# Output projection: 512 columns and 128 tokens to a PSUM bank, in place of 256 columns and two times 128 tokens

## The chip, the cores and the metric

The kernel runs on one core of one Trainium2 chip. The metric is the device time of one execution in microseconds, from the first instruction to the last. Three runs of the kernel before gave 1098.61, 1100.31 and 1105.79 us; the median is 1100.31. The trace that is quoted here is that of another, profiled execution of the same kernel.

## What is computed

One layer of a hybrid encoder, on a prompt of 1024 tokens and a sample of 512 tokens, both of width 1024. A combined projection feeds a Hyena branch (short convolution, long convolution by transforms, gates) and a branch of neighbourhood attention with 8 heads of 64. Each branch gives 512 channels, and the layer ends in one output projection over both:

```python
def encoder_layer(x, norm_g, w_in, ...):
    h = rmsnorm(x, norm_g)
    z = h @ w_in
    ...
    y_hy = x0 * long_conv(x1 * vv, kfilt, hy_bias)
    y_hy = rmsnorm(y_hy, on_hy) * jax.nn.silu(hy_gate)
    ...
    y_att = neighbourhood_attention(q, k, v, rpb)
    y_att = rmsnorm(y_att, on_att) * jax.nn.silu(att_gate)
    return x + jnp.concatenate([y_hy, y_att], axis=-1) @ w_out
```

The change is in the last line alone. All values are float32.

## The kernel before

**Precision.** Products that need float32 are made of three matmuls on rounded halves: every operand is split into `hi` (rounded) and `lo` (the rest), and the sums hi x hi, hi x lo and lo x hi add up in PSUM. So each weight piece and each operand is loaded as float32, copied to `hi` (VectorE or ScalarE) and subtracted to `lo` (GpSimd).

**Stages.** The program goes through normalising and turning x, then the prompt's projections together with the filters' spectra, the prompt's Hyena, the prompt's attention together with the sample's Hyena, and last the output projection together with the sample's attention (`run`, lines 1148 to 1253). Within a stage, generators are traced in turns (`weave`, line 347) and a scheduler then sets the order of instructions on each engine by priorities; the attention of the sample has priority 4000 over the outputs. Each engine works in its order, so what waits at the head of its queue holds up all behind it. All DMAs are issued by SyncE (`dma`, line 58).

**The output projection** (`out_part`, lines 1078 to 1136). It runs in passes: part 0 multiplies the four channel blocks (k = 0 to 3, 128 channels each) of the Hyena output by their rows of `w_out`, part 1 does it for the attention. A job is 512 tokens: two jobs of the prompt and one of the sample. Part 0 of the prompt's two jobs comes first, then their part 1, then part 0 of the sample, and after the sample's attention has ended, part 1 of the sample. At the start of a pass each job loads its four operand blocks from scratch in DRAM (`lo<-A_p`, `lo<-A_s`, line 1089), ScalarE copies them to `hi` (line 1090) and GpSimd subtracts (`lo`, line 1091 through the helper at line 63). The operands have one tile per job and block, so part 1's loads wait until part 0 has let the tile go.

The loop inside (lines 1095 to 1136) takes 256 output columns at a time (g = 0 to 3). For each job and each pair of 128-token tiles it fills one PSUM bank of 512 float32: 4 blocks x 2 tiles x 3 matmuls of 256 columns = 24 matmuls. The token tile is the stationary operand, the weights stream:

```python
for g in range(4):                                                     # 1095
    ...
    units = [... self.take_w(("w_out", g, part)) ... for _ in range(2)]  # 1097
    for jb in jobs:
        ...
        for t in (0, 2):
            ps = self.bank(next(self.mm_tags)).rearrange("p (a c) -> p a c", a=2)
            for k in range(4):
                ...
                for j in range(2):
                    ...
                    for i, (w, h) in enumerate(((whi, hi), (wlo, hi), (whi, lo))):
                        nc.tensor.matmul(ps[:, j, :], lhsT=h[:, tok], rhs=w, ...)   # 1111
```

Then the bank is evicted, half by half. In job 0 and the sample's job VectorE adds it, scaled by each token's norm factor, to an accumulator in SBUF that was filled with x by DMA (`acc`, line 1133 through the helper at line 75). The prompt's second job has no accumulator: in part 0 ScalarE scales the bank (`oo`, line 1123) and a DMA writes it to DRAM scratch (`sum`), in part 1 `sum` and x come back (`oy`, `ox`), GpSimd adds them and VectorE adds the bank. In part 1 a DMA writes the output.

**The weights.** A piece is 128 partitions x 1024 columns (512 KB); for `w_out` that is 4 blocks x 256 columns. `fetch_w` (line 344 and after, DMA at line 351) loads it into one of two `wraw` tiles of a pool, `issue_w` (lines 354 to 367) splits it into two units of 512 columns, each with a `whi` (line 365) and a `wlo` (GpSimd, line 366), of which a pool has four each. `take_w` (line 369) hands units out in order and issues further pieces as far as there is room: `w_bufs` is 4 until part 0 of the prompt's jobs is done, then 8, and pieces go by turns to a second pool with the same number of tiles. One step of the loop over g uses one piece, two units.

**Attention of the sample** (line 894 and after). For each of 8 heads a table comes by DMA (`qkr<-in_rpb_dram`) and GpSimd makes two tables of it (`T`, then `Ti`). For each unit TensorE makes the scores (lines 994 and 995), VectorE and ScalarE the softmax, TensorE transposes (line 1020) and multiplies by the values (line 1029), ScalarE and VectorE put the result together (`ya`, lines 1033 and 1034). At the end of a pair of heads `finish` (line 1036) loads a gate (`qkr<-ga_s`), multiplies (line 1046) and stores the block to scratch (`A_s<-ya`). The row sums over channels (line 828) give the norm factors of part 1.

## Time and profile before

| | |
|---|---|
| median of three runs | 1100.31 us (1098.61 to 1105.79) |
| span of the profiled execution | 1101.3 us (the profile shows no time around it) |
| TensorE busy in it | 1030.7 us, 94%, 6492 matmuls |
| VectorE, ScalarE, GpSimd busy | 824.4, 561.1, 539.9 us |
| granted TensorE clock, mean | 0.987 of 2.4 GHz |
| DMA | 154.87 MB, 44.3% of the span of 16 engines |
| matmuls of the output projection (line 1111) | 1152, from 883.9 us to 1097 us |

The profile is one execution. A busy TensorE is not TensorE at its peak: matmuls are pipelined and their ends are modelled, so the distance between starts is the better measure. A wait is put down to the engine that released it last.

### The profile page before, as it was taken

How to read it: one execution, taken by the hardware profiler on the slowest of the kernel's cores; microseconds unless marked ns; L12 is line 12 of the kernel's file. 1: busy time of each engine (PE TensorE's matmuls, PEld its weight loads, DVE VectorE, ACT ScalarE, POOL GpSimd, SP SyncE). 2: the span in 40 equal slices, each digit the busy share in tenths (PEclk: the TensorE clock that was granted, in tenths of full speed). 3: DMA queues.
4: the chain of work that ended last, by engine and by line, in shares of the span. 5: the costliest groups of instructions: out<-in, count | busy, mean ns of one | idle time of the engine just before them, and what ended most of it. 6: DMA issues, size and time to landing. Idle time of an engine off the chain costs nothing. (4 is left out here: it accounts for less than half of the span.)

```text
span 1101.3 us, 18549 instructions
## 1 busy us (share of the span) xinstructions
PE 1030.7 (94%) x6492; PEld 895.6 (81%) x6492; DVE 824.4 (75%) x2098; ACT 561.1 (51%) x1223; POOL 539.9 (49%) x480
## 2 busy tenths in 40 slices
PE   3999898998999999999898999999999999899998
PEld 2888887987888878787786887888777798798898
DVE  5988679456148597868768898999886868966874
ACT  6644616444534343443425577667567764564530
POOL 2133636325245474545445645455455564766452
PEclk9999999899999999999999899999999999999999
DMA  9134461645612121122375244445544376966522
GB/s 343 34 122 144 143 207 61 219 150 164 224 39 74 46 79 54 50 72 77 118 227 173 78 129 146 120 141 182 140 129 138 114 243 190 321 203 205 164 76 89
DMA packets 110780, 154.87 MB, mean 141 GB/s; under 512 B 7793, under 2 KB 80315, under 8 KB 109919
## 3 DMA queue, kind: packets, MB, share of 16 engines
q1 hardware_dynamic: 110687, 153.69, 44.3%
q8 instruction: 51, 0.84, 0.3%
q14 instruction: 42, 0.34, 0.1%
HBM read 110.35 MB, written 43.32 MB: 140 GB/s over the span
## 5 line engine op out<-in xcount | busy, mean ns | idle before, releaser
L366 POOL TENSOR_TENSOR wlo<-wraw,whi 128x512 fp32r<-128x512 f32 x160 | 231.5, 1451 | 308.4 <-ACT whi L365 180.7
L392 PE MATMUL bank<-hThi_p,whi 128*128 128x512 f32 x320 | 125.2, 391 | 2.0 <-DVE cx L75 2.0
L392 PE MATMUL bank<-hTlo_p,whi 128*128 128x512 f32 x320 | 125.5, 392 | 0.0
L392 PE MATMUL bank<-hThi_p,wlo 128*128 128x512 f32 x320 | 125.4, 392 | 0.0
L405 PE MATMUL bank<-whi,hThi_p 128*128 128x256 f32 x384 | 110.4, 290 | 2.5 <-ACT qsq L849 2.0
L1111 PE MATMUL bank<-whi,hi 128*128 128x256 f32 x384 | 111.0, 291 | 0.8 <-ACT hi L1090 0.5
L405 PE MATMUL bank<-wlo,hThi_p 128*128 128x256 f32 x384 | 110.8, 291 | 0.0
L1111 PE MATMUL bank<-wlo,hi 128*128 128x256 f32 x384 | 110.0, 288 | 0.0
L1111 PE MATMUL bank<-whi,lo 128*128 128x256 f32 x384 | 109.5, 289 | 0.3 <-POOL lo L63 0.3
L405 PE MATMUL bank<-whi,hTlo_p 128*128 128x256 f32 x384 | 108.1, 289 | 0.0
L450 POOL TENSOR_TENSOR Z<-zc,Z 128x256 fp32r<-128x256 f32 x80 | 69.5, 878 | 49.2 <-ACT Z L449 36.2
L1002 ACT ACTIVATE s_sb<-s_sb,mx 128x360 f32<-128x360 f32 (+1 forms) x96 | 60.4, 629 | 63.6 <-DVE mx L998 63.0
L405 PEld LDWEIGHTS bank<-whi,hThi_p 128*128 128x128 f32 x384 | 74.2, 194 | 4.9 <-ACT qsq L849 2.4
L1111 PEld LDWEIGHTS bank<-whi,hi 128*128 128x128 f32 x384 | 73.4, 191 | 4.1 <-issue 2.1
L405 PEld LDWEIGHTS bank<-wlo,hThi_p 128*128 128x128 f32 x384 | 74.5, 194 | 1.6 <-issue 0.7
L1111 PEld LDWEIGHTS bank<-wlo,hi 128*128 128x128 f32 x384 | 73.6, 192 | 1.6 <-issue 1.6
L1111 PEld LDWEIGHTS bank<-whi,lo 128*128 128x128 f32 x384 | 73.1, 192 | 1.7 <-issue 1.1
L405 PEld LDWEIGHTS bank<-whi,hTlo_p 128*128 128x128 f32 x384 | 73.3, 194 | 1.2 <-issue 0.7
L392 PEld LDWEIGHTS bank<-hThi_p,whi 128*128 128x128 f32 x320 | 60.3, 188 | 14.0 <-DVE cx L75 2.4
L392 PEld LDWEIGHTS bank<-hTlo_p,whi 128*128 128x128 f32 x320 | 60.4, 189 | 11.3
L392 PEld LDWEIGHTS bank<-hThi_p,wlo 128*128 128x128 f32 x320 | 60.3, 188 | 11.3
L392 PE MATMUL bank<-hThi_s,whi 128*128 128x512 f32 x160 | 64.6, 407 | 4.4 <-DVE cvv L75 2.3
(292 smaller groups left out, 3108.4 us busy)
## 6 DMA issues: line engine op xcount, KB each, us to landing
wraw<-in_w_ch_dram SPq DMA_DIRECT2D x40, 512.0 KB
wraw<-in_w_tk_dram SPq DMA_DIRECT2D x24, 512.0 KB
wraw<-in_w_out_dram SPq DMA_DIRECT2D x16, 512.0 KB
V<-v_p SPq DMA_DIRECT2D x32, 240.0 KB
v_p<-vg SPq DMA_DIRECT2D x32, 160.0 KB
K_p<-Kw SPq DMA_DIRECT2D x4, 1088.0 KB
x<-in_x_prompt_dram SPq DMA_DIRECT2D x8, 512.0 KB
dec<-in_dec_p_dram SPq DMA_DIRECT2D x16, 256.0 KB
```

Source lines behind the costliest of these rows:

```text
L366: nc.gpsimd.tensor_tensor(out=lo, in0=r, in1=f32(hi), op=ALU.subtract)
L392: nc.tensor.matmul(ps, lhsT=w, rhs=h[s][:, k], start=(k == 0 and i == 0), stop=(k == KC - 1 and i == 2))
L405: nc.tensor.matmul(pss[t // 2][:, t % 2, :], lhsT=h[t // 4][:, k, t % 4 * P:(t % 4 + 1) * P], rhs=w, start=(k == 0 and i == 0 and t % 2 == ...
L450: nc.gpsimd.tensor_tensor(out=Z[:, 1, 0:2, :], in0=z, in1=f32(Z[:, 0, 0:2, :]), op=ALU.subtract)
L1002: nc.scalar.activation(out=s_sb[:, :n], in_=s_sb[:, :n], func=AF.Exp, bias=mx, scale=-1.0, accum_out=l)
L1111: nc.tensor.matmul(ps[:, j, :], lhsT=h[:, tok], rhs=w, start=(k == 0 and i == 0 and j == 0), stop=(k == 3 and i == 2 and j == 1))
```

## The change

A bank now holds one tile of 128 tokens and 512 output columns: 4 blocks x 3 matmuls of 512 columns = 12 matmuls in place of 24. The loop goes over two halves (h) of the output columns. Each half takes four units at its start, one unit per block k (512 columns of one block), and keeps them until its last tile. With two jobs, job 0 does its four tiles in the first step of the half and job 1 in the second, where before both jobs took turns in each of the four steps; with one job a step has two tiles. A bank is evicted by one operation of 512 columns. The piece of weights is now 2 blocks x 512 columns and is put together by two DMAs of 256 KB, since the weights lie in DRAM as before. Accumulators are filled with x by two loads of 1 MB in place of four of 512 KB. The number of banks (48) and the bytes are the same. Comments and docstrings also go.

```diff
         if what[:3] == "out":
-            return [[]] + [[("w_out", g, int(what[3]))] for g in range(4)]
+            return [[]] + [[("w_out", h, int(what[3]), u)] for h in range(2) for u in range(2)]
...
+    def load_w(self, raw, key):
+        if key[0] != "w_out":
+            self.dma(raw, self.io[key[0]][key[1:]])
+            return
+
+        _, h, part, u = key
+        for g in range(2):
+            self.dma(raw.rearrange("p (k g c) -> p k g c", k=2, g=2)[:, :, g],
+                     self.io["w_out"][h * 2 + g, part].rearrange("p (k c) -> p k c", k=4)[:, u * 2:u * 2 + 2])
+
     def fetch_w(self):
...
-            self.dma(raw, self.io[key[0]][key[1:]])
+            self.load_w(raw, key)
...
-        for g in range(4):
-            gs = slice(g * 256, (g + 1) * 256)
-            units = [[t.rearrange("p (k c) -> p k c", c=256) for t in self.take_w(("w_out", g, part))] for _ in range(2)]
...
+        for h in range(2):
+            hs = slice(h * 512, (h + 1) * 512)
+            units = [self.take_w(("w_out", h, part, k // 2)) for k in range(4)]
+            for step in range(2):
+                for jb in (jobs if len(jobs) == 1 else jobs[step:step + 1]):
+                    for t in (range(4) if len(jobs) > 1 else range(step * 2, step * 2 + 2)):
+                        self.out_tile(part, jb, t, hs, units)
+                yield
+
+    def out_tile(self, part, jb, t, hs, units):
+
+        nc = self.nc
+        G, acc = jb["G"], jb.get("acc")
+        t += jb["seg"] * 4
+        rows = slice(t * P, (t + 1) * P)
+        r = (G.ratt if part else G.rhy)[:, t:t + 1]
+        t %= 4
+        if part == 0 and acc and t == 0:
+            t0 = jb["seg"] * 4
+            self.dma(acc[:, :, hs], G.x[t0 * P:(t0 + 4) * P, hs].rearrange("(t p) c -> p t c", p=P))
+        ps = self.bank(next(self.mm_tags))
+        tok = slice(t * P, (t + 1) * P)
+        for k, (whi, wlo) in enumerate(units):
+            hi, lo = jb["hi"][k][:, tok], jb["lo"][k][:, tok]
+            for i, (w, a) in enumerate(((whi, hi), (wlo, hi), (whi, lo))):
+                nc.tensor.matmul(ps, lhsT=a, rhs=w, start=(k == 0 and i == 0), stop=(k == 3 and i == 2))
+        if acc:
+            o = acc[:, t, hs]
+        elif part == 0:
+            o = jb["first"].tile([P, 512], F32, name="oo", bufs=2)
+            nc.scalar.mul(out=o, in_=ps, mul=r)
+            self.dma(self.sum_d[rows, hs], o)
+            return
+        else:
+            o = jb["last"].tile([P, 512], F32, name="oy", bufs=3)
+            self.dma(o, self.sum_d[rows, hs])
+            x = jb["last"].tile([P, 512], F32, name="ox", bufs=3)
+            self.dma(x, G.x[rows, hs])
+            self.add(o, o, x, nc.gpsimd)
+        self.stt(o, ps, r, o)
+        if part == 1:
+            self.dma(G.out[rows, hs], o)
```

Up to the last stage the order of instructions on each engine is the same. Within it the scheduler orders anew. Two places matter here.

The first is GpSimd near the start of the stage, where the sample's attention makes its first tables (`T`, `Ti`) and the weights of part 0 are split (`wlo`). Before, this stands on GpSimd:

```order
L366 TENSOR_TENSOR wlo<-wraw,whi 128x512
L909 MEMSET T_10667 128x2x40
L909 MEMSET T_10670 128x2x40
L955 MEMSET kst 128x64 x2
L666 TENSOR_TENSOR Y<-yA,Y 128x256
L955 MEMSET kst 128x64
L63 TENSOR_TENSOR T_10667<-cmask,qkr 128x480
L63 TENSOR_TENSOR T_10670<-cmask,qkr 128x480
L366 TENSOR_TENSOR wlo<-wraw,whi 128x512
L63 TENSOR_TENSOR Ti_10669<-T_10667,rmask 128x360
L63 TENSOR_TENSOR Ti_10672<-T_10670,rmask 128x360
L366 TENSOR_TENSOR wlo<-wraw,whi 128x512
```

And this stands there now:

```order
L965 MEMSET kst 128x64
L676 TENSOR_TENSOR Y<-yA,Y 128x256
L965 MEMSET kst 128x64 x2
L63 TENSOR_TENSOR T_10669<-cmask,qkr 128x480
L63 TENSOR_TENSOR T_10672<-cmask,qkr 128x480
L376 TENSOR_TENSOR wlo<-wraw,whi 128x512
L63 TENSOR_TENSOR Ti_10671<-T_10669,rmask 128x360
L376 TENSOR_TENSOR wlo<-wraw,whi 128x512
L63 TENSOR_TENSOR Ti_10674<-T_10672,rmask 128x360
L376 TENSOR_TENSOR wlo<-wraw,whi 128x512 x2
```

Before, one split stood ahead of the tables and one each before and behind the first `Ti` operations. Now the splits that belong to the second half of part 0, four of them, all stand behind the two `T` operations.

The second is the end of SyncE's queue. `A_s_106` to `A_s_109` are the four blocks of the sample's attention in scratch; `ya` is such a block, stored from SBUF; `ga_s_113` is the last gate. `lo` with four running numbers (13042 to 13045 before, 12534 to 12537 now) are the operands of part 1 of the sample. Before:

```order
L60 DMA A_s_108<-ya 128x512
L60 DMA wraw<-in_w_out_dram 128x1024
L60 DMA V<-v_s_124 120x3x128
L60 DMA V<-v_s_125 120x3x128
L60 DMA qkr<-ga_s_113 128x512
L60 DMA A_s_109<-ya 128x512
L60 DMA lo_13042<-A_s_106 128x512
L60 DMA lo_13043<-A_s_107 128x512
L60 DMA lo_13044<-A_s_108 128x512
L60 DMA lo_13045<-A_s_109 128x512
L60 DMA out_dram<-acc 128x2x256 x8
```

Now:

```order
L60 DMA A_s_108<-ya 128x512
L60 DMA V<-v_s_124 120x3x128
L60 DMA V<-v_s_125 120x3x128
L60 DMA lo_12534<-A_s_106 128x512
L60 DMA lo_12535<-A_s_107 128x512
L60 DMA lo_12536<-A_s_108 128x512
L60 DMA qkr<-ga_s_113 128x512
L60 DMA A_s_109<-ya 128x512
L60 DMA lo_12537<-A_s_109 128x512
L60 DMA out_dram<-acc 128x512 x8
```

Three of the four operand loads moved ahead of the last gate's load and of the last store of the attention; all four stood behind that store before. The last load of weights went further to the front.

## Rows read from the trace of the kernel before

**Rows 1.** The page, its first part: busy us (share of the span) x instructions.

```profile
span 1101.3 us, 18549 instructions
...
PE 1030.7 (94%) x6492; PEld 895.6 (81%) x6492; DVE 824.4 (75%) x2098; ACT 561.1 (51%) x1223; POOL 539.9 (49%) x480
```

**Rows 2.** Line 1111: matmuls, min/median/max ns, first and last start us.

```profile
L1111 PE MATMUL bank<-whi,hi x384: 274/283/420, 883.9 to 1096.7; 128*128 128x256 f32 x192
```

**Rows 3.** Busy us by stretch (start:end, length, then each engine).

```profile
core 0: us, PE busy (x) PEld busy (x) DVE busy (x) ACT busy (x) POOL busy (x), PEclk, DMA share, GB/s
925.00:975.00 50.00, 44.23 (x297) 37.70 (x296) 42.60 (x102) 29.46 (x69) 36.43 (x33) 0.97 0.97 292
975.00:1065.00 90.00, 88.72 (x674) 81.78 (x674) 65.11 (x168) 42.83 (x101) 50.84 (x48) 1.00 0.50 154
```

**Rows 4.** The chain that ended last: start us, us, what.

```profile
946.39 10.84 DMA acc<-in_x_sample_dram
...
1070.56 0.80 PE bank L828 x8
...
1073.94 8.65 PE bank L1111 x68
...
1082.60 14.66 PE bank L1111 x120
```

**Rows 5.** Timeline of the end: start us, us, engine, line, what.

```profile
1083.06 0.28 PE L1111 MATMUL bank<-whi,hi 128*128 128x256 f32 x1
...
1083.41 0.28 PE L1111 MATMUL bank<-whi,hi 128*128 128x256 f32 x1
...
1083.41 0.19 PEld L1111 LDWEIGHTS bank<-wlo,hi 128*128 128x128 f32 x1
...
1085.81 0.28 PE L1111 MATMUL bank<-whi,lo 128*128 128x256 f32 x1
```

**Rows 6.** Timeline of TensorE, the sample's projections.

```profile
867.32 0.39 PE L392 MATMUL bank<-hTlo_s,whi 128*128 128x512 f32 x1
...
871.88 0.39 PE L392 MATMUL bank<-hThi_s,whi 128*128 128x512 f32 x1
```

**Rows 7.** Groups by shape, 884 to 1101 us: busy us, mean ns | idle before.

```profile
L366 POOL TENSOR_TENSOR wlo<-wraw,whi 128x512 fp32r<-128x512 f32 x28 | 37.3, 1336 | 32.0 <-DVE whi L365 27.8 <-DVE rs_t L63 3.8 <-DVE rl L1004 0.4
...
L75 DVE SCALAR_TENSOR_TENSOR acc<-bank,ra_s,acc 128x256 f32<-128x256 f32 x16 | 6.8, 478 | 10.5 <-PE bank L1111 10.5
...
L75 DVE SCALAR_TENSOR_TENSOR kst<-bank,pc,kst 64x512 fp32r<-64x512 f32 x8 | 6.0, 750 | 1.8 <-ACT kst L949 1.6
```

**Rows 8.** Timeline of all engines around the last attention output.

```profile
1064.17 0.76 PE L1029 MATMUL bank<-pt,V 120*64 120x256 f32 x5
...
1065.37 0.43 DVE L63 TENSOR_TENSOR ya<-bank,ya 64x256 f32<-64x256 f32 x1 [0.80 <-ACT ya L1033]
...
1068.04 0.74 DVE L75 SCALAR_TENSOR_TENSOR ya<-ya,pc,qkr 128x512 f32<-128x512 f32 x1
...
1068.81 0.34 SPq L60 DMA_DIRECT2D A_s<-ya  x1
...
1069.75 3.36 SPq L60 DMA_DIRECT2D lo<-A_s  x4
...
1072.37 1.29 ACT L1090 CAST hi<-lo 128x512 fp32r<-128x512 f32 x2 [5.91 <-DMA lo<-A_s]
...
1075.96 0.62 ACT L1090 CAST hi<-lo 128x512 fp32r<-128x512 f32 x1 [0.62 <-DMA lo<-A_s]
```

**Rows 9.** Timeline of GpSimd at the first tables.

```profile
920.64 2.42 POOL L63 TENSOR_TENSOR T<-cmask,qkr 128x480 f32<-128x480 f32 x2 [5.09 <-DMA qkr<-in_rpb_dram]
...
923.02 1.33 POOL L366 TENSOR_TENSOR wlo<-wraw,whi 128x512 fp32r<-128x512 f32 x1
```

**Rows 10.** Timeline of TensorE, 914 to 928 us.

```profile
919.14 0.28 PE L1111 MATMUL bank<-whi,lo 128*128 128x256 f32 x1
...
927.85 0.30 PE L763 MATMUL bank<-ident,s 128*128 128x128 f32 x1 [1.71 <-DVE s L63]
```

More of the change, by code (lines that the diff above doesn't have):

```diff
@@ L1094, in out_part @@
         yield
-        for g in range(4):
-            gs = slice(g * 256, (g + 1) * 256)
-            units = [[t.rearrange("p (k c) -> p k c", c=256) for t in self.take_w(("w_out", g, part))] for _ in range(2)]
-            for jb in jobs:
-                G, t0, acc = jb["G"], jb["seg"] * 4, jb.get("acc")
-                if part == 0 and acc:
-                    self.dma(acc[:, :, gs], G.x[t0 * P:(t0 + 4) * P, gs].rearrange("(t p) c -> p t c", p=P))
-                r = G.ratt if part else G.rhy
-                for t in (0, 2):
-                    ps = self.bank(next(self.mm_tags)).rearrange("p (a c) -> p a c", a=2)
-                    for k in range(4):
-                        whi, wlo = [u[:, k % 2, :] for u in units[k // 2]]
-                        hi, lo = jb["hi"][k], jb["lo"][k]
-                        for j in range(2):
-                            tok = slice((t + j) * P, (t + j + 1) * P)
-                            for i, (w, h) in enumerate(((whi, hi), (wlo, hi), (whi, lo))):
-                                nc.tensor.matmul(ps[:, j, :], lhsT=h[:, tok], rhs=w,
-                                                 start=(k == 0 and i == 0 and j == 0), stop=(k == 3 and i == 2 and j == 1))
-                    def rows(d, t=t, t0=t0):
-                        return d[(t0 + t) * P:(t0 + t + 2) * P, gs].rearrange("(t p) c -> p t c", p=P)
-                    rs = [r[:, t0 + t + j:t0 + t + j + 1] for j in range(2)]
-                    if acc:
-                        o = acc[:, t:t + 2, gs]
-                    elif part == 0:
-                        o = jb["first"].tile([P, 2, 256], F32, name="oo", bufs=2)
-                        for j in range(2):
-                            nc.scalar.mul(out=o[:, j], in_=ps[:, j], mul=rs[j])
-                        self.dma(rows(self.sum_d), o)
-                        continue
-                    else:
-                        o = jb["last"].tile([P, 2, 256], F32, name="oy", bufs=3)
-                        self.dma(o, rows(self.sum_d))
-                        x = jb["last"].tile([P, 2, 256], F32, name="ox", bufs=3)
-                        self.dma(x, rows(G.x))
-                        self.add(o, o, x, nc.gpsimd)
-                    for j in range(2):
-                        self.stt(o[:, j], ps[:, j], rs[j], o[:, j])
-                    if part == 1:
-                        self.dma(rows(G.out), o)
-            yield
```

## Prediction

> **What bounds the kernel now.** I read the page's first part, then the view of line 1111, then busy time and granted clock by stretch, the chain of work that ended last, and the timeline of the engines that the change touches. The span is 1101.3 us with TensorE busy 94% [rows 1]. That share is only a hint, since matmul ends are modelled and overlap. The change touches the last stage alone: the matmuls of line 1111 run from 883.9 us to 1097 [rows 2], some 213 of the 1101 us. By stretch [rows 3], from 925 to 975 us the DMA engines are 97% busy and TensorE is idle for 5.8 of 50 us, at a mean clock of 0.97; from 975 to 1065 TensorE is busy for 88.7 of 90 us at its full 2.4 GHz. The chain agrees [rows 4]: near 946 it runs through a load, x of the sample, for 10.84 us, and it ends with 120 matmuls of line 1111 in one piece. So TensorE sets the time of this stage, but for a few microseconds in its first half.
>
> Then the pace, which busy time hides. In the unbroken end, matmuls of 256 columns start at 1083.41 and, 20 later, at 1085.81: 2.40 / 20 = 0.120 us each, though each row is 0.28 long and its weight load 0.19 [rows 5]. Loads and streams overlap, and the distance between starts is what a matmul costs. The 512-column matmuls of line 392 start at 867.32 and, 20 later, at 871.88: 0.228 us each [rows 6].
>
> **The change part by part.**
>
> *Columns.* 1152 matmuls of 256 columns become 576 of 512 on the same data: 1152 x 0.120 = 138.2 us becomes 576 x 0.228 = 131.3, 6.9 us less. With the mean of the last piece of the chain (14.66 / 120 = 0.122, [rows 4]) it is 9.2 less; with the 0.117 of the three starts from 1083.06 to 1083.41 [rows 5], 3.5. I take -6.9, the value of the longest unbroken row of starts, and keep -3.5 and -9.2 as ends. Half the weight loads go; they were covered by streaming, so by themselves they give nothing.
>
> The Trainium skill speaks against so much. In "TensorE: Matmul & The Clock Gate", section "Back-to-back issue gap", a warm matmul costs its columns over 2.4 GHz plus 2.5 ns. As an estimate from that page, two of 256 columns take 218.3 ns and one of 512 takes 215.7, and this part would be worth 576 x 2.6 ns = 1.5 us. The trace does not agree: 120 ns against the page's 109 for 256 columns, 228 against 216 for 512.
>
> *Evictions.* Five of the six passes evict through VectorE, with one operation of 512 columns where there were two of 256. Two cost 2 x 0.478 = 0.96 us; the nearest 512-column row out of PSUM takes 0.75 [rows 7]. So 40 x 0.21 = 8 us of VectorE go, which is busy for 42.6 of 50 us at worst and for 65 of 90 in the long middle [rows 3], where TensorE sets the pace. I cost it at 0; it is worth up to 2 us where VectorE's queue holds up the attention, and less than nothing nowhere, as the work shrinks. On the path stands the last eviction alone: -0.2. The number of banks stays at 48, so there are no more waits for a free one.
>
> *DMAs.* Each of the 16 weight pieces comes by two DMAs of 256 KB, and x comes into the accumulators by half as many loads of twice the size: 16 issues more and 4 fewer. At 0.34 us an issue [rows 8] that is 4 us of SyncE over 213. I take 0, since pieces are fetched ahead; if all 16 second issues delayed a step it would be 5.4. The bytes are the same. The big loads of x for the sample move behind loads of part 1's operands and weights in SyncE's queue, and the first of them is what the chain waits for near 946 [rows 4]. Of the 5.8 idle us of that stretch [rows 3] I take 2 off, with 0 and -5.8 as ends.
>
> *Weights of half a pass at once.* Before, a step holds two of the four weight buffers, and the next two are split meanwhile. Now half a pass holds all four until its last tile, and until the second pool opens the next four have no room. The first such place is between the halves of part 0. There GpSimd now has all four splits behind two table operations, which wait 5.09 us for a DMA: these start at 920.64 and take 2.42, and the first split ends at 924.3 [rows 9]. Before, two later splits stood there too, but TensorE lived on pieces split earlier; it started the 192nd matmul of the stage (the end of the first half) at 919.14 [rows 10]. With three transforms of hyena's (0.4) TensorE gets to 919.6, and has one matmul (0.2) and the first scores (0.6) to go on with: 924.3 - 919.6 - 0.8 = 3.9 us idle. But it was idle for 1.7 us before 927.85, waiting for hyena on VectorE [rows 10], and that wait now falls into the same delay: +2.2 net. The ends are 0, if the table's data lands earlier, and +5.1, its whole wait, if nothing covers it. Queued behind the blocked splits on GpSimd are the next tables and the operands of part 1, and TensorE waits for both. The second place is from part 0 to part 1: at most four splits less the last tile, 4 x 1.34 [rows 7] - 12 x 0.228 = 2.6 us. Two tiles share each split there and attention stands between, so +1 of 0 to +2.6. After that each pool holds half of a step, and the next is split in time.
>
> *The end.* Part 0 of the sample now ends before attention's last values. So three of the last part's four operands are loaded before the last output of attention is stored, and 27 matmuls come ahead of those that need the fourth. Before, 250 matmuls of 256 columns (30 us) follow the last value group, which ends at 1064.93 [rows 8]; now it is 92 of 512, 21 us. The difference is no gain by itself, since what moves forward lengthens the time before; the sum over the columns holds it. New is a wait. From the last values to the fourth operand, by [rows 8]: 0.9 us to the end of the values' sum (1065.80), 0.74 for the gated product, 7.15 from the store's issue (1068.81) to the cast that follows the load (1075.96), 0.62 for that cast: 9.4 us. TensorE has 23 matmuls (5.2) and the row sums (0.8, [rows 4]) ahead of it: 3.4 us idle. A shorter wait stands just before: the first operand's load waits for its tile, 9 matmuls (2.1 us) before TensorE wants it, and load and cast take 2.6 + 0.65 [rows 8]: 1.2 us. Before, the stretch from 1071.36 to 1073.94, where the chain runs over VectorE [rows 4], held 15 matmuls (1.8 us): 0.8 lost. Net 3.4 + 1.2 - 0.8 = +3.8, from 0 (if TensorE comes to it late) to +6 (if the product waits in VectorE's queue as it did before, 2.2 us).
>
> **Sum.** -6.9 - 0.2 - 2 + 2.2 + 1 + 3.8 = -2.1 us on a span of 1101.3. The page shows no time around the span; the median of the three timed runs is 1100.31, 1 us from it and inside their spread of 7. So 1100.3 - 2.1, rounded to 1098 us. All low ends together give -17, all high ends +17.
>
> **The rivals.** *Faster: the waits don't appear and the load-bound stretch shrinks.* If hyena and attention fill TensorE at the two places and at the end, -6.9, -0.2 and the full -5.8 remain: 1100.3 - 12.9, about 1087. For it: scores and values of the attention stand between the tiles at each place. Against it: between the last values and the fourth operand nothing else is left to do.
>
> *No change: the columns are hidden anyway.* From 925 to 975 the DMA engines set the pace [rows 3], and at the end the store and load of the last operand do; saved columns then turn into idle time, and the end comes at 1100 to 1102. For it: the 3.4 us at the end. Against it: 90 us in the middle in which TensorE is idle for 1.3 in all [rows 3]. A pace of 512 columns that falls short of [rows 6], as in the output's own setting with banks changing every 12, ends here too. By the rule of "TensorE: Matmul & The Clock Gate" in the Trainium skill the sum would, as an estimate, be 5.4 us higher, near 1104.
>
> *Slower: weights come late at each place without room.* GpSimd takes its work in order. If the splits of a half pass fall behind a table's DMA, the place costs the wait, two table operations and four splits, 5.09 + 2.42 + 5.34 = 12.9 us [rows 7, 9], less the last tile's 2.7: 10 us. At two places that is 20, and with -6.9, -0.2, -2 and +3.8 some 15 us more: 1115. It decides the sign once both places together cost over 5 us, and makes over 1% from 16 us on. For it: GpSimd's order. Against it: tables and splits then wait at a time when TensorE has attention to do.
>
> **How the numbers follow.** I give the forecast 0.52, the faster rival 0.16, no change 0.22, the slower one 0.10. About 1% (11 us) is what a measurement of this kernel tells from no change. The forecast and no change lie inside it: 0.74 within; 0.16 faster, 0.10 slower. The range is 1086 to 1110: it takes in the faster rival and stops short of the slower one, which leaves less than 2 in 10 out.
>
> **What would show it.** Right: starts 0.228 us apart in the output's matmuls; TensorE idle for 3 to 5 us near 920 with the weight split as releaser; idle again for some 3 us before the fourth operand's matmuls, with ScalarE's cast as releaser; the last 60 matmuls in one piece of 13.7 us; less idle time from 940 to 965. Wrong: another pace of these matmuls, idle stretches at later half passes, or a last value group more than 6 us away from 1065.

## The result, and the profile after

| | before | after |
|---|---|---|
| median of the runs made side by side, us | 1099.46 (1096.84 to 1105.79, 4 runs) | 1110.31 (1109.86 to 1115.58, 4 runs) |
| ratio, 95% interval | | 1.0104 [1.0067, 1.0141] |
| profiled execution, span us | 1101.3 | 1108.9 |

The changed kernel is about 1% slower; the forecast was 1098 us, in a range of 1086 to 1110. In its lines, 1130 is the output's matmul (1111 before), 1135 ScalarE's eviction, 1100 the cast of an operand, 375 and 376 the two halves of a weight split, 838 the row sums.

The page's first part (busy us, share of the span, instructions) hides it, as [rows 1] did: TensorE is as busy as before with 576 instructions fewer. In part that is so because a matmul counts as busy for longer at half the clock (0.63 us for 512 columns, where it is 0.39 at the full clock).

```profile
span 1108.9 us, 17344 instructions
...
PE 1031.0 (93%) x5916; PEld 865.5 (78%) x5916; DVE 825.9 (74%) x2058; ACT 559.8 (50%) x1215; POOL 538.1 (49%) x480
```

The stretches say more (busy us by engine, granted clock, share of the DMA engines' time):

```profile
core 0: us, PE busy (x) PEld busy (x) DVE busy (x) ACT busy (x) POOL busy (x), PEclk, DMA share, GB/s
884.00:925.00 41.00, 37.01 (x185) 29.32 (x185) 28.91 (x63) 19.31 (x41) 23.08 (x27) 0.96 0.57 188
925.00:975.00 50.00, 41.57 (x196) 31.44 (x195) 43.35 (x93) 27.93 (x64) 37.59 (x33) 0.92 0.85 258
975.00:1065.00 90.00, 87.05 (x402) 66.91 (x401) 57.10 (x131) 37.70 (x87) 45.47 (x43) 0.97 0.51 161
1065.00:1109.00 44.00, 37.06 (x169) 29.32 (x168) 23.22 (x49) 7.58 (x17) 14.23 (x11) 0.94 0.25 88
```

Against [rows 3], TensorE from 925 to 975 us is idle for 8.4 us where it was 5.8, at a mean clock of 0.92 where it was 0.97, and the DMA engines move 258 GB/s where they moved 292. From 975 to 1065, 1.3 us idle have become 3.0. The stretches don't hold quite the same work: this execution came to the first matmul of the stage at 880.0 us, 3.9 us earlier than the one before, through stages that the change leaves as they were.

One number per kernel makes this comparable. From 870 us to the last matmul I took the distance from each matmul's start to the next one's, less the usual distance of its kind (0.120 us for 256 columns of the output, 0.2275 for 512, the 30th percentile in the trace of before for other kinds). What is over counts as clock where the granted clock is 1.2 GHz, up to one more usual distance, and as waiting otherwise. The sums hang on what is taken as usual; the differences between kernels hardly do. By stretch, waiting and clock together:

| us | 870-910 | 910-930 | 930-970 | 970-990 | 990-1010 | 1010-1030 | 1030-1070 | from 1070 | sum (of it clock) |
|---|---|---|---|---|---|---|---|---|---|
| before | 3.0 | 3.3 | 8.8 | 1.0 | 0.9 | 2.2 | 2.1 | 1.4 | 22.8 (1.5) |
| after | 3.3 | 6.7 | 11.8 | 5.1 | 0.9 | 5.9 | 2.1 | 5.9 | 41.7 (8.2) |

So 18.9 us more were lost, 6.7 of them by the clock, and 1152 x 0.120 - 576 x 0.2275 = 7.2 us gained on the columns: +11.7 us for the stage. Its matmuls start over 224.7 us where they did over 213.1. The spans of the two traces differ by 7.6 us only, as the changed kernel's came to the stage 3.9 us earlier; the medians differ by 10.9.

What the waits are is read at five places. The first is the one that the prediction named. GpSimd, then TensorE:

```profile
915.52 2.35 POOL L63 TENSOR_TENSOR T<-cmask,qkr 128x480 f32<-128x480 f32 x2 [5.29 <-DMA qkr<-in_rpb_dram]
917.83 1.31 POOL L376 TENSOR_TENSOR wlo<-wraw,whi 128x512 fp32r<-128x512 f32 x1
```

```profile
919.19 0.66 PE L1130 MATMUL bank<-wlo,hi 128*128 128x512 f32 x1 [2.83 <-POOL wlo L376]
```

A table's load holds up the tables, these hold up the weight split, and TensorE waits 2.83 us for the split. The second place was not named. ScalarE, VectorE, GpSimd and TensorE, 940 to 951 us (in brackets the idle time before, and who ended it):

```profile
943.94 0.62 ACT L1100 CAST hi<-lo 128x512 fp32r<-128x512 f32 x1 [6.34 <-DMA lo<-A_s]
```

```profile
940.99 0.16 DVE L63 TENSOR_TENSOR rs_t<-rs_t,rs_h 128x4 f32<-128x4 f32 x1
945.18 0.16 DVE L1014 RECIPROCAL rl<-l 128x1 f32<-128x1 f32 x1 [4.04 <-ACT s_sb L1012]
945.26 0.61 DVE L81 TENSOR_SCALAR rs_t<-rs_t 128x4 f32<-128x4 f32 x1
945.91 1.12 DVE L63 TENSOR_TENSOR rs_y<-rs_y,rs_t 128x4 f32<-128x4 f32 x1
947.06 1.28 DVE L63 TENSOR_TENSOR rs_t<-rs_y 128x4 f32<-128x4 f32 x1
948.37 1.18 DVE L63 TENSOR_TENSOR rs_t<-rs_t,rs_h 128x4 f32<-128x4 f32 x1
949.48 0.74 DVE L75 SCALAR_TENSOR_TENSOR acc<-bank,rh_p,acc 128x512 f32<-128x512 f32 x1
```

```profile
945.05 0.80 POOL L63 TENSOR_TENSOR Ti<-T,rmask 128x360 f32<-128x360 f32 x1
945.80 1.21 POOL L63 TENSOR_TENSOR T<-cmask,qkr 128x480 f32<-128x480 f32 x1
...
947.05 2.48 POOL L63 TENSOR_TENSOR lo<-lo,hi 128x512 fp32r<-128x512 f32 x2
```

```profile
950.27 0.79 PE L1130 MATMUL bank<-whi,hi 128*128 128x512 f32 x1 [3.51 <-DVE acc L75]
```

Read it from below. TensorE wants a bank that VectorE has to evict. VectorE stood 4.04 us waiting for ScalarE's softmax, and then did four small operations that take 4.2 us in all, beside GpSimd's large ones; ScalarE stood 6.34 us at the cast of an operand that had not landed.

The third place is the change from part 0 to part 1, where the 7 us from 965.5 hold four waits of TensorE. From 950 to 975, VectorE is busy for 23.23 of 25 us (19.80 before), GpSimd for 22.25 (18.77 before). The stretch, VectorE, then TensorE:

```profile
950.00:975.00 25.00, 20.90 (x86) 15.45 (x87) 23.23 (x48) 14.01 (x32) 22.25 (x18) 0.84 0.90 280
```

```profile
963.61 1.43 DVE L375 CAST whi<-wraw 128x512 fp32r<-128x512 f32 x1
964.97 0.15 DVE L1014 RECIPROCAL rl<-l 128x1 f32<-128x1 f32 x1
965.04 1.42 DVE L375 CAST whi<-wraw 128x512 fp32r<-128x512 f32 x1
966.38 1.33 DVE L79 TENSOR_SCALAR s_sb<-s_sb,rl 128x360 f32<-128x360 f32 x1
```

```profile
967.86 0.52 PE L1030 MATMUL bank<-ident,s_sb 128*120 128x128 f32 x3 [1.86 <-DVE s_sb L79]
```

TensorE waits for the softmax, and the softmax stands on VectorE between casts of weights, which take 1.42 us beside GpSimd's half of the split and 0.42 without it (six of the eight casts of this stretch take 0.98 us or more).

The fourth place is the end:

```profile
1084.33 1.05 PE L838 MATMUL bank<-ones,sqs 128*128 128x1 f32 x8 [0.29 <-POOL sqs L63]
1087.20 0.79 PE L1130 MATMUL bank<-whi,hi 128*128 128x512 f32 x1 [1.82 <-ACT hi L1100]
...
1091.22 0.51 PE L1130 MATMUL bank<-whi,hi 128*128 128x512 f32 x1 [0.37 <-DVE acc L75]
```

That is the predicted wait for the fourth operand. Between the third place and the end lies a fifth, 1010 to 1030 us, where 3.7 us more are lost than before. GpSimd, VectorE, TensorE:

```profile
1015.73 1.28 POOL L63 TENSOR_TENSOR oy<-oy,ox 128x512 f32<-128x512 f32 x1 [4.02 <-DMA oy<-sum]
...
1023.19 2.36 POOL L63 TENSOR_TENSOR T<-cmask,qkr 128x480 f32<-128x480 f32 x2 [4.92 <-DMA qkr<-in_rpb_dram]
```

```profile
1024.42 0.53 DVE L1008 CUSTOM_DVE_ANT_0 s_sb<-bank,T 128x360 f32<-128x360 f32 x1 [1.44 <-POOL T L63]
```

```profile
1025.02 1.00 PE L955 MATMUL bank<-ident,qkr 128*128 128x128 f32 x4 [1.28 <-DVE mx L1008]
```

GpSimd stands for sums that come back from DRAM, then for a table; VectorE's pass over the scores waits for the table, and TensorE waits for VectorE.

The chain of what ended last holds, from 937 us on, loads of operands, the load of the sample's x (in the chain before too, [rows 4]), the way of the sums through DRAM, a table's load, and the last piece of 60 matmuls, 13.91 us long where [rows 4] had 120 in 14.66:

```profile
937.69 9.12 DMA lo<-A_s
946.88 5.51 DMA lo<-A_p
952.40 10.69 DMA acc<-in_x_sample_dram
...
1009.96 5.71 DMA oy<-sum
1018.29 4.74 DMA qkr<-in_rpb_dram
...
1091.22 13.91 PE bank L1130 x60
```

### The profile page after: what moved, and what is told of

Read it like the earlier page. It is cut to its first block, busy times and chain, and to the rows that moved or that the text cites. A ratio compares the mean times of both kernels' runs of the same rounds, so it can differ in the third digit from the quotient of the medians.

```text
span 1108.9 us, 17344 instructions
## 1 busy us (share of the span) xinstructions
PE 1031.0 (93%) x5916; PEld 865.5 (78%) x5916; DVE 825.9 (74%) x2058; ACT 559.8 (50%) x1215; POOL 538.1 (49%) x480
## 4 chain that ended last, share of the span: by engine, by line
PE 48%; DVE 16%; DMA 8%; ACT 4%; issue 4%; POOL 2%; SPq 1%; DVEq 0%; POOLq 0%; ACTq 0%
PE bank L402 20%; PE bank L1130 8%; PE bank L415 6%; PE bank L1039 3%; PE bank L1030 2%; PE bank L1005 2%; PE bank L471 2%; DMA v_p<-vg 2%; PE bank L472 2%; PE bank L473 2%; DVE zc L63 1%; DVE whi L375 1%; SPq L60 1%; DMA lo<-A_s 1%; DVE bt L63 1%
## 5 line engine op out<-in xcount | busy, mean ns | idle before, releaser
L376 POOL TENSOR_TENSOR wlo<-wraw,whi 128x512 fp32r<-128x512 f32 x160 | 229.1, 1438 | 286.4 <-ACT whi L375 179.3
L1130 PE MATMUL bank<-whi,hi 128*128 128x512 f32 x192 | 80.2, 420 | 6.3 <-DVE acc L75 4.3
L1130 PE MATMUL bank<-wlo,hi 128*128 128x512 f32 x192 | 78.9, 413 | 2.8 <-POOL wlo L376 2.8
L1130 PE MATMUL bank<-whi,lo 128*128 128x512 f32 x192 | 77.7, 412 | 0.6 <-POOL lo L63 0.6
L375 DVE CAST whi<-wraw 128x512 fp32r<-128x512 f32 x94 | 62.0, 666 | 10.4 <-PE bank L402 8.4
L63 POOL TENSOR_TENSOR T<-cmask,qkr 128x480 f32<-128x480 f32 x32 | 39.7, 1249 | 59.2 <-DMA qkr<-in_rpb_dram 57.0
L1039 PE MATMUL bank<-pt,V 120*64 120x256 f32 (+1 forms) x352 | 67.0, 299 | 1.1 <-ACT pt L1032 0.7
```

Of the source, the lines that this page charges most:

```text
L63: (eng or self.nc.vector).tensor_tensor(out=out, in0=a, in1=b, op=op)
L375: next(self.w_round)(out=hi, in_=r)
L376: nc.gpsimd.tensor_tensor(out=lo, in0=r, in1=f32(hi), op=ALU.subtract)
L1039: nc.tensor.matmul(o, lhsT=vl, rhs=pr_, start=(c == 0 and i == 0), stop=(c == ncu - 1 and i == 1))
L1130: nc.tensor.matmul(ps, lhsT=a, rhs=w, start=(k == 0 and i == 0), stop=(k == 3 and i == 2))
```

## The experiments

The times are medians, each with its ratio to the kernel before on the same chip (there 1100.2 to 1100.4 us).

**The weights.** My first theory: half a pass holds all four weight units, and the next have no room. One run opens the second pool from the start of the stage; the other holds four units in the kernel before.

```diff
-        self.weave(self.chain(self.out_part(0, jobs[:2]), self.then(more_w), self.out_part(1, jobs[:2]), self.out_part(0, jobs[2:])),
+        more_w()
+        self.weave(self.chain(self.out_part(0, jobs[:2]), self.out_part(1, jobs[:2]), self.out_part(0, jobs[2:])),
```

> The changed kernel with the second weight pool open from the start of the output stage, so that half a pass can be split while the other is used. Theory (weights of half a pass held at once leave no room, the gaps at the two early half passes follow, and after each gap the clock is at half): the gaps near 916 to 919 and 963 to 972 us go, with the half-clock stretches behind them; 4 to 7 us less than the changed kernel, about 1104. Rival (order of the jobs and the scratch round trip make the gaps): no change, about 1110.

```diff
-            units = [... self.take_w(("w_out", g, part)) ... for _ in range(2)]
+            if g % 2 == 0:
+                both = [[... self.take_w(("w_out", g + n, part)) ... for _ in range(2)] for n in range(2)]
+            units = both[g % 2]
```

> The kernel before, but the weights of two steps (four units) are taken together at every second step; 256 columns, pairs of tiles, turns of the jobs and the DMAs of before stay. Theory (holding four units of four makes the loss): 8 to 16 us more than before, about 1110. Rival (the order of the jobs or the evictions make it): within 3 us of before, about 1100.

Measured: 1116.42 us, 1.0157 [1.0127, 1.0188], and 1101.22 us, 1.001 [0.9987, 1.0032]. The theory fell twice: more room made the changed kernel slower, and holding four units costs the kernel before nothing clear of noise. The second run is the cleaner one, as in the first the order of everything else moved too (its trace has TensorE at 1.2 GHz for 37 us, see the end of this document).

**The columns, in the changed kernel's order.**

```diff
-                nc.tensor.matmul(ps, lhsT=a, rhs=w, ...)
+                for c in range(2):
+                    cs = slice(c * 256, c * 256 + 256)
+                    nc.tensor.matmul(ps[:, cs], lhsT=a, rhs=w[:, cs], ...)
```

> The changed kernel, each matmul of 512 columns made as two of 256 on the same operands; weights, order of the jobs and evictions as in the changed kernel. Theory (the columns are worth what the spacing of starts says, the loss is elsewhere): 5 to 9 us more than the changed kernel, about 1117. Rival (512 columns gain nothing or make the loss): the same as the changed kernel or less, 1110 or below.

Measured: 1107.99 us, 1.0076 [1.0049, 1.0102]. So 512 columns win nothing there. With them undone 32.2 us go to waits and clock, where the changed kernel loses 41.7: what the columns save, waits eat.

**The order of the jobs.** The rival: before, both prompt jobs take turns in each step; the change runs four tiles of job 0, then four of job 1.

```diff
-                for jb in (jobs if len(jobs) == 1 else jobs[step:step + 1]):
-                    for t in (range(4) if len(jobs) > 1 else range(step * 2, step * 2 + 2)):
+                for jb in jobs:
+                    for t in range(step * 2, step * 2 + 2):
```

> The changed kernel, but both jobs of the prompt take turns in each step, two tiles each, as they did before. Theory: weights are held as long as in the changed kernel, so the gaps stay: within 4 us of it, 1106 to 1114. Rival (one job after the other makes the gaps, by evictions and scratch loads that come in a bunch): 6 to 12 us less, about 1100.

Measured: 1099.81 us, 0.9995 [0.9981, 1.001]. Turns take the whole loss away: 10.5 us. The weights are held as long as in the changed kernel, and the wait for the weight split near 920 us is still there:

```profile
920.60 0.79 PE L1130 MATMUL bank<-wlo,hi 128*128 128x512 f32 x1 [2.85 <-POOL wlo L376]
```

By the measure above, taken on both traces alike, turns lose 10.8 us less: some 4 each at 970 to 990 and at 1010 to 1030, some 2 each from 930 to 970 and from 1070, and 2 more than job order from 1030 to 1070. Then turns in one part alone, and the two jobs exchanged (`jobs[1 - step:2 - step]`):

> The changed kernel with the two prompt jobs taking turns (two tiles each per step) in part 0 alone; part 1 stays in job order. Turns in both parts gave 1099.8 us, job order in both 1110.3. If part 0 is where job order costs (a bunch of four evictions through VectorE while it converts scores, and a bunch of four through ScalarE behind the operand casts), this run ends at 1100 to 1103. If it is part 1 (a bunch of four tiles that read the stored sums and x, with three buffers), it ends at 1107 to 1111. If both share it, near 1105.

> The mirror: turns in part 1 alone, part 0 in job order. If part 0 is where job order costs: 1107 to 1111, with the idle stretch near 946 still there. If part 1: 1100 to 1103, with the idle stretch of 1020 to 1025 gone. If both share it: near 1105.

> The changed kernel with the jobs of each half pass in the opposite order: job 1 (evicted by ScalarE, summed through DRAM) first, then job 0. A control: if what costs is that four tiles of one job follow one another, whichever comes first, this stays at 1107 to 1114. If it is only where job 0's accumulator load and VectorE's evictions happen to fall, it moves by more than 5 us to either side (below 1105 or above 1115).

Measured: 1103.91 us, 1.0037 [1.0014, 1.006]; 1110.53 us, 1.0094 [1.0058, 1.0129]; 1115.78 us, 1.0136 [1.0107, 1.0165]. So turns in part 0 alone give back 6.4 us, a little less than was expected, and turns in part 1 alone nothing; once part 0 takes turns, part 1's turns are worth another 4.1. Exchanging the jobs is 5 us worse still, just past the bound that was set for a pure matter of four in a row: where the bunch falls counts too. Tile by tile, in place of two tiles each:

> The kernel whose jobs take turns, with turns tile by tile in place of two tiles each, so that VectorE's and ScalarE's evictions alternate at every bank. If the bunching of one engine's evictions still costs at two tiles: 1094 to 1098. If two tiles are as good: 1098 to 1102.

Measured: 1105.8 us, 1.0064 [1.0044, 1.0084], slower than two by two. So it isn't simply that evictions of one engine stand in a row.

**The columns, with turns.** The edit of two matmuls of 256, in the kernel that takes turns:

> The kernel in which the jobs take turns (1099.8 us), with each matmul of 512 columns made as two of 256. Theory: with the order mended, the columns are worth what the pace says, about 7 us of TensorE's work; as that kernel's waits at its end and the time at 1.2 GHz eat some of it, 1102 to 1107. Rival: 512 columns are worth nothing here, since TensorE that is done sooner only waits longer and falls to 1.2 GHz more often: 1098 to 1101.

Measured: 1109.92 us, 1.0081 [1.0051, 1.0111]. With turns, 512 columns are worth 10.1 us, more than their work. This run is also the changed kernel's half passes without the columns and without the order of the jobs. It is 9.5 us slower than the kernel before, and loses 30.0 us to waits and clock, 7.2 more: 1.8 of it at 910 to 930, 3.9 at 970 to 990, 3.1 from 1070. Holding four units cost the kernel before 1 us (above). What else the half passes cost here (the pieces, the banks of one tile, the loads of x, the scheduler's order) no run tells apart.

**Two DMAs to a piece.** `w_out` laid out so that a piece is one DMA of 512 KB, with turns:

> The kernel whose jobs take turns (1099.8 us), with w_out laid out so that each piece of weights comes by one DMA of 512 KB in place of two of 256 KB. Theory: 16 issues of 0.34 us on SyncE are hidden, 1098 to 1101. Rival: the second issue of a piece delays the loads behind it in the load-bound stretch, and without it 1093 to 1097.

Measured: 1101.92 us, 1.0017 [0.9998, 1.0035]. The second issues are hidden, as the prediction took them.

**ScalarE's casts.** To test the chain at 946, the four casts of the sample's Hyena operands go to GpSimd, in job order and with turns:

```diff
-                nc.scalar.copy(out=hi, in_=a)
+                if part == 0 and len(jobs) == 1:
+                    nc.gpsimd.tensor_copy(out=hi, in_=a)
+                else:
+                    nc.scalar.copy(out=hi, in_=a)
```

> The changed kernel (job order), with the four casts of the sample's hyena operands made by GpSimd in place of ScalarE. In the changed kernel ScalarE stands 6.3 us at such a cast until the operand has landed, the softmax waits behind it, VectorE waits 4.0 us for the softmax, and TensorE 3.5 us for a bank that VectorE is to evict. Theory: that chain is the first part of what job order costs. The idle stretch near 946 goes, with the fall of the clock behind it: 1104 to 1107. Rival: the loads set the pace of this stretch whoever casts, and the wait moves to another place: 1109 to 1113.

> The same move of the four casts in the kernel whose jobs take turns (1099.8 us). There ScalarE stands 2.4 us at the cast and no wait of VectorE or TensorE over 0.3 us follows from it. Theory: nothing to win, 1098 to 1102. Rival: the casts cost something in this order too, and 1094 to 1097 comes out; or GpSimd, which then has 4 us more work among weight splits, makes it slower: 1103 to 1107.

Measured: 1114.15 us, 1.0142 [1.0111, 1.0174], and 1108.8 us, 1.0093 [1.006, 1.0127]. Both are slower than without the move, by 3.8 and 9.0 us. The idle stretch near 946 is gone in the first, yet the time isn't. TensorE's waits have moved on by 20 us, behind three casts of weights on VectorE (VectorE, then TensorE):

```profile
962.31 4.24 DVE L375 CAST whi<-wraw 128x512 fp32r<-128x512 f32 x3
```

```profile
967.05 0.44 PE L1004 MATMUL bank<-kst,qhh 128*128 128x360 f32 x1 [2.28 <-DVE mx L1008]
967.42 0.43 PE L1005 MATMUL bank<-kst,qlo 64*128 64x360 f32 x1
968.67 0.58 PE L1039 MATMUL bank<-pt,V 120*128 120x256 f32 x1 [0.82 <-ACT pt L1032]
970.21 1.12 PE L1039 MATMUL bank<-pt,V 120*64 120x256 f32 x4 [0.96 <-DVE pt L63]
```

The chain stands in the trace, but taking ScalarE's cast out of it wins nothing. The move also gives GpSimd four more operations, so it does not show what the chain alone costs.

**The loads.** Without the loads of x for job 1 (`ox`), in both orders; x is then missing from that half of the prompt's output. They are 8 loads and 2.1 MB, not 16 and 4 MB as the expectations say:

```diff
-            x = jb["last"].tile([P, 512], F32, name="ox", bufs=3)
-            self.dma(x, G.x[rows, hs])
-            self.add(o, o, x, nc.gpsimd)
+            self.add(o, o, o, nc.gpsimd)
```

> The changed kernel (job order) without the 16 loads of x for job 1 in part 1 (4 MB; GpSimd adds the sum to itself in their place, so that its work stays; x is left out of that half of the prompt's output). Some six of these loads stand between 922 and 949 us, among the operands that ScalarE's casts wait for. Theory: what job order costs is the loads coming in a worse order in a stretch in which the DMA engines are busy 99%. With these bytes gone the waits of ScalarE for the operand go below 3 us, the idle stretches near 946 and 965 to 972 shrink to under 3 us together, and the time is 1098 to 1103. Rival: the order of the jobs costs by itself, by VectorE's evictions standing in a row: 1107 to 1111.

> The same 16 loads left out of the kernel whose jobs take turns (1099.8 us); the control to the run above. Theory: turns hid most of the loads' order already, so it gains less than the other: 1095 to 1098, 3 to 5 us below job order without these loads. If job order costs by the loads alone, the two kernels without them come within 2 us of one another; if by the evictions, the distance stays at 10 us.

Measured: 1106.77 us, 1.0062 [1.0045, 1.0079], and 1104.73 us, 1.0037 [1.002, 1.0054]. The two kernels come to 2.0 us from one another, as the theory of the loads wanted, but not where it wanted them: with 2.1 MB less to load, the kernel that takes turns became 4.9 us slower. This is inconclusive. A likely reason, not shown, is that leaving out one kind of instruction also changes the order that the scheduler gives the others.

**The end.** First without the fourth operand's wait, by loading the third in its place (the sample's output is then another):

```diff
-                self.dma(a, self.A_d[G.name][part * 4 + k][:, sl])
+                last = part == 1 and len(jobs) == 1 and k == 3
+                self.dma(a, self.A_d[G.name][6 if last else part * 4 + k][:, sl])
```

> The changed kernel (job order), with the last part's fourth operand read from the third operand's row of attention's output, so that it needn't wait for the last values (the output of the sample is then another). The same loads, casts and matmuls. Theory: the wait at the end, put at 3.4 + 1.2 - 0.8 = 3.8 us in the prediction, and 1.3 us for the fall of the clock behind it, go: 1105 to 1108. Rival: another wait takes its place, the third operand's or the row sums', 1109 to 1112.

Measured: 1113.61 us, 1.0127 [1.0103, 1.0151]. It is 3.3 us slower. Another wait stood behind the first, that of the row sums, as the rival had it, and it is longer. TensorE and VectorE of this run:

```profile
1085.44 0.95 PE L838 MATMUL bank<-ones,sqs 128*128 128x1 f32 x8
1090.62 0.79 PE L1131 MATMUL bank<-whi,hi 128*128 128x512 f32 x1 [4.23 <-DVE acc L75]
```

```profile
1086.42 0.16 DVE L839 COPY ra_s<-bank 128x4 f32<-128x4 f32 x1 [5.03 <-PE bank L838]
...
1089.61 0.17 DVE L843 COPY ra_s<-rs_y 128x4 f32<-128x4 f32 x1
1089.82 2.07 DVE L75 SCALAR_TENSOR_TENSOR acc<-bank,ra_s,acc 128x512 f32<-128x512 f32 x3
```

All three banks are full and can't be evicted: the eviction multiplies by the row scale `ra_s`, which needs the row sums of the last attention output and then 17 small operations, from 1086.42 to 1089.78. So the end seems to lack banks. Six of them for the last part (three of attention's, which is done), with turns:

```diff
+        self.mm_tags = itertools.cycle(["mm", "tp", "mo", "tp", "mm", "tp"])
         self.weave(self.out_part(1, jobs[2:]))
```

> The kernel whose jobs take turns (1099.8 us), with the last part's matmuls cycled over six banks, three of them those of attention's transposes, which are done by then. So 54 of its matmuls have no need of the fourth operand, in place of 27, 6 us more to go on with. Theory: the wait for the fourth operand (1.9 us idle and 1.4 us at half the clock) goes: 1096 to 1098, and a kernel faster than before by 0.2 to 0.4%. Rival: something else ends last (the row sums, the weights of the second half pass) and it stays at 1099 to 1101.

Measured: **1095.23 us, 0.9951 [0.9934, 0.9969]**, 5.1 us faster than the kernel before, and 4.6 us faster than with three banks. TensorE and VectorE show why:

```profile
1075.02 0.95 PE L838 MATMUL bank<-ones,sqs 128*128 128x1 f32 x8
1075.83 0.49 PE L1130 MATMUL bank<-whi,hi 128*128 128x512 f32 x1
```

```profile
1079.20 0.17 DVE L843 COPY ra_s<-rs_y 128x4 f32<-128x4 f32 x1
1079.48 4.93 DVE L75 SCALAR_TENSOR_TENSOR acc<-bank,ra_s,acc 128x512 f32<-128x512 f32 x7
```

TensorE goes on behind the row sums without a wait, and VectorE, once the scale is there, makes seven evictions in a row. The same line in the kernel before and in the changed kernel:

> The kernel before, with its last part's matmuls cycled over six banks in place of three; the control to the run of turns with six banks (1095.2). Before, 250 matmuls follow the last values and only 1.4 us are lost between 1070 and the end. Theory: little to win, 1098 to 1100, so that what turns with six banks gained is the columns' and not the banks'. Rival: three banks cost the kernel before as much, and 1094 to 1096 comes out.

> The changed kernel (job order) with the same six banks. It loses 4.6 us between 1070 and the end and 1.3 us there by the fall of the clock. Theory: taking only the operand's wait away gained nothing, as evictions then wait for the row scale with three banks full; with six banks both waits are covered, and 4 to 6 us go: 1104 to 1106.5. What is left over 1100 is then the order of the jobs. Rival: the lost time moves on to the weights of the second half pass, 1108 to 1111.

Measured: 1099.69 us, 0.9999 [0.9976, 1.0021], and 1107.67 us, 1.0059 [1.0037, 1.008]. The kernel before has nothing to win by banks; in its trace 248 matmuls of the output still follow the last values, which fits. The changed kernel loses only 0.5 us from 1070 on, where it lost 5.9, and wins 2.6 in the median, less than expected: in its trace more is lost at 970 to 990 (7.2 us for 5.1).

## Why the prediction was wrong

*The columns.* Right as a pace: starts 0.227 to 0.229 us apart in unbroken rows (predicted 0.228), 7.2 us of work less (predicted 6.9), and with turns 10.1 us of time. In job order they were worth nothing, which is the rival "hidden anyway", at another place than it said.

*The step that failed: the sum holds no term for the order of the jobs.* The prediction priced columns, evictions, DMAs, weights and the end; that a step now runs four tiles of one job, with nothing of the other between, is in none of its terms. Turns against job order make 10.5 us in the changed kernel, 12.4 with six banks, 5.4 with the casts on GpSimd, 2.0 without `ox`, and -1.9 with 256 columns; in part 0 alone it is 6.4 (part 1 in job order) or 10.7 (part 1 in turns). So it is a cost of 512 columns in this order, and its size hangs on what else lies in the stretch. That the order of the jobs makes the loss of this kernel is shown; by which waits is shown only in part. One chain stands in the trace (a bank that VectorE evicts late, behind ScalarE at a cast), but moving the cast off it moved the wait and won nothing, and that stretch holds only some 2 of the 10.8 us by which turns lose less. More lies behind the change of parts and at 1010 to 1030. From 950 to 975 the trace points to VectorE, 93% busy (85% with turns), with casts that last longer beside GpSimd (six of eight over 0.9 us; with turns three of eight), and at 1010 to 1030 to sums and tables that GpSimd waits for. No run took either cause away alone: they are argued, not shown. It stays open, too, how much of each distance is the scheduler's order of everything else.

*The clock.* It had no term either, and 6.7 of the 18.9 us are clock. At the end of the idle stretches named above, or in them, the records show 1.2 GHz from 919.4 (3.4 us), 950.1 (3.4), 970.6 (6.8), 1025.2 (3.4) and 1086.6 (3.4); before, up to the last matmul, only from 929.3 (3.4). So the clock added half as much again to the 12.2 us of waiting that were new.

*Weights of half a pass.* The first place is right: idle for 2.83 us with the split as releaser (predicted 3.9 gross, 2.2 net). But the kernel that takes turns has that wait too, 2.85 us, and comes out level with the kernel before. The second was put at +1; at 970 to 990 the changed kernel lost 4.1 us more than before, and not as it was put: TensorE waits for the softmax, which stands behind the weights' casts on VectorE, and then runs at 1.2 GHz; it does not wait for the weights. In the run without columns and order the 3.9 us of that stretch are again no wait for weights: TensorE stands 2.12 us before a matmul of attention's values, whose releaser the profile doesn't name. So holding half a pass at once is not shown to cost what these terms priced, and the slower rival (weights late at each place, 1115) has the direction right but not the cause. The load-bound stretch (930 to 970) should have shrunk by 2 and grew by 3.0.

*The end.* Sized right (+3.8; from 1070 on 4.5 more were lost), by half a reason. The wait for the fourth operand is there, with ScalarE's cast as releaser and the last 60 matmuls in one piece of 13.91 us (predicted 13.7). But taking it away gained nothing: in that run three banks full of sums without their row scale stopped TensorE for 4.23 us.

*The sum.* With turns and 512 columns the time is 1099.8, within 2 us of the 1098 that was forecast, so the prediction was one of that kernel; but it is near by luck. The half passes with 256 columns and turns cost 9.5 us, where the terms without columns and last eviction make +5.0, and the columns gave 10.1, where 6.9 was put: two errors that cancel. The high ends as they are listed add up to some +15, not +17, which changes no chance. The last values ended 13 us later than before, not within 6, with most of the waits ahead of them.

## What to carry to other kernels

A change that halves the number of passes also changes who follows whom: write down, for each wait of the profile, what used to stand between its two ends, and give the new order a term of its own, with the fall of the clock behind each wait. Work that TensorE saves is only worth something where TensorE is what the stretch waits for; test that by undoing the saving in the order as it is. When sums must wait for a scale that comes last, more banks cover the wait; here, with turns, that one line made a change without gain into a kernel 0.5% faster.

## What the runs showed of the hardware

**VectorE beside GpSimd.** The row scale's operations on 128x4 elements take 0.16 us in the rows above while GpSimd stands idle (940.99) and, for the three with two operands, 1.12 to 1.28 us while GpSimd works on operands of 128x480 and 128x512. The Trainium skill, "SBUF — State Buffer", section "Who interferes with whom", says that a VectorE instruction with two SBUF inputs contends with a GpSimd instruction that reads SBUF, and that the lock on the ports they share is exclusive. The trace agrees: each of the three ends within 0.05 us of an instruction of GpSimd's (1.2 to 1.3 us long), whatever its own size. The one with a single operand, 0.61 us, ends with GpSimd's 945.05 in the same way. Here the four together held a bank's eviction for 4.2 us.

**The clock and the time of an execution go together.** In the 12 timed executions of the changed kernel with six banks, the mean granted clock goes from 0.986 to 0.975 while the time goes from 1100.55 to 1109.95 us (correlation -0.90, 0.89 us for each 0.001). In the 23 executions of the kernel before beside them it is -0.73 and 0.59 us. Means of 0.9866 for these and 0.9795 for the changed kernel's four make 0.0071, so by these slopes 4 to 6 of its 10.9 us go with the clock. As the clock falls at waits, this counts waits too, and no run sets the clock by itself. And 1.2 GHz can last. With the second pool opened early, TensorE has no output matmul from 915 to 954 us. Between a wait of 5.79 us before 925.29 and one of 4.35 before 952.59 it does matmuls of the other work, its longest wait there 1.03 us, and the records show half the clock for 37 us:

```profile
905.00:920.00 15.00, 12.89 (x64) 10.04 (x62) 9.32 (x27) 8.31 (x15) 4.02 (x6) 1.00 0.47 146
920.00:957.00 37.00, 23.43 (x77) 16.81 (x77) 31.91 (x71) 17.73 (x40) 25.93 (x25) 0.50 0.81 254
957.00:985.00 28.00, 28.00 (x135) 21.96 (x135) 17.56 (x43) 15.96 (x37) 13.62 (x14) 0.99 0.61 172
```
